# Summing the last row of a row-sum kernel by two pair adds on VectorE, with the first sum carried into the second

## The chip, the cores and the metric

The kernel runs on one core of one Trainium2 chip. The metric is the device time of one execution in microseconds (us), lower is better. A row holds 1,024 fp32 numbers.

## The reference

```python
batch, seq, dim = 32, 512, 1024
x = np.random.randn(batch, seq, dim).astype(np.float32)

def reference(x):
    return np.sum(x, axis=-1).astype(np.float32)
```

16,384 rows are summed: 67.1 MB are read and 64 KB are written. Each of the 128 partitions gets 128 rows, in four blocks of 32.

## The kernel before

Seven tiles of 16 rows per partition are loaded and summed, nearly all on VectorE. The last 16 rows come in shrinking pieces (8, 4, 2 and 1 rows, then the last row in 640 and 384 elements), so that little work is left when the last byte lands. VectorE and ScalarE share these pieces.

```python
    def sum_act(v, acc):                       # ScalarE: sum of v into acc
        nc.scalar.activation(out=v, in_=v, func=COPY, accum_out=acc)

    def row_pairs_dve(xt, res, j, c):          # VectorE: 512 pairs of one row
        h = D // 2
        a, b = xt[:, j * D : j * D + h], xt[:, j * D + h : (j + 1) * D]
        nc.vector.tensor_tensor_reduce(
            out=a, in0=a, in1=b, scale=1.0, scalar=0.0, op0=ADD, op1=ADD,
            accum_out=res[:, c : c + 1],
        )
    # ... (seven tiles of 16 rows; loads of 8, 4, 2 and 1 rows into xt) ...
    nc.sync.dma_start(out=tail[:, 0:CUT], in_=x_b[:, last : last + CUT])          # CUT = 640
    nc.sync.dma_start(out=tail[:, CUT:D], in_=x_b[:, last + CUT : last + D])
    # ... (8 + 4 rows, halved between VectorE and ScalarE) ...
    i = cuts[2]
    rows_dve(xt, res, i, 1, c + i)                      # row 12: VectorE
    rows_act(xt, res, i + 1, 1, c + i + 1)              # row 13: ScalarE
    row_pairs_dve(xt, res, i + 2, c + i + 2)            # row 14: VectorE, by pairs
    nc.vector.tensor_reduce(                            # row 15, first 320
        out=tail[:, D : D + 1], in_=tail[:, 0 : CUT // 2], axis=X, op=ADD
    )
    sum_act(tail[:, CUT // 2 : CUT], tail[:, D + 1 : D + 2])   # row 15, next 320
    nc.vector.tensor_reduce(                            # row 15, 384 + the two sums
        out=res[:, n - 1 : n], in_=tail[:, CUT : D + 2], axis=X, op=ADD
    )
    nc.sync.dma_start(out=out_b, in_=res)
```

## Time and profile before

| | before |
|---|---|
| time, median of 3 | 163.21 us (163.21 to 163.22) |
| the profiled execution | 163.75 us, span 162.0 us |
| read | 67.11 MB at 415 GB/s over the span |
| VectorE / ScalarE busy | 76% / 10% |

The page of the kernel before, its busy time and the share of the data movers in 40 slices of the span (a digit is the busy share in tenths):

```profile
DVE 123.5 (76%) x14; ACT 15.8 (10%) x29; POOL 0.2 (0%) x4
...
DMA  7979989989979969969959959969969959999991
```

The loads run nearly from start to end, and VectorE waits for each full tile (2.1 to 2.5 us for each after the first, by its timeline). What can still be shortened by compute is mainly the time between the landing of the last bytes and the issue of the final store.

The timeline of the last microseconds (start, length, engine, line, operation; in brackets the idle time before and what ended it):

```profile
157.86 0.69 DVE L57 CUSTOM_DVE_ANT_0 xt<-xt 128x512 f32<-128x512 f32 x1
158.48 0.08 DVE L57 DVE_READ_ACCUMULATOR2_ANT res<- 128x1 f32 x1
158.58 0.47 ACT L48 ACTIVATE tail<-tail 128x320 f32<-128x320 f32 x1 [0.97 <-DMA tail<-in_x_dram]
158.58 0.49 DVE L102 TENSOR_REDUCE tail<-tail 128x1 f32<-128x320 f32 x1
158.95 0.19 ACT L48 ACTIVATION_READ_ACCUMULATOR tail<-tail 128x1 f32 x1
159.17 0.55 DVE L106 TENSOR_REDUCE res<-tail 128x1 f32<-128x386 f32 x1
159.75 0.35 SPq L109 DMA_DIRECT2D out_dram<-res  x1
```

```profile
122.25 36.30 DMA tail<-in_x_dram
158.55 0.02 issue
158.58 0.47 ACT tail L48
159.05 0.10 ACTq L135
159.15 0.02 issue
159.17 0.55 DVE res L106
```

The first piece of the last row lands at 158.55 us, ScalarE sums half of it, and only then can VectorE's last reduction start. The second piece, by the trace's record of its landing at 159.014 us, is there earlier than ScalarE's sum. The store is issued at 159.75, that is 0.740 us after the last landing. This distance, from the last landing to the store's issue within one trace, is the first measure used below: it hardly depends on how the stream ran before (0.740 and 0.732 us in two traces of this kernel whose spans differ by 0.5 us; before_copy, below).

### The profile page before, as it was taken

What the parts mean: (1) busy time and instruction counts of PE and PEld (TensorE: products, weight loads), DVE (VectorE), ACT (ScalarE), POOL (GpSimd) and SP (SyncE); (2) the same over time, 40 slices, a digit from 0 to 9 for tenths busy, and PEclk for the clock granted to TensorE, in tenths of its full rate; (3) what the DMA queues carried; (4) which work ended last, traced back from release to release, by engine and by line L of the source; (5) the groups of instructions that cost most, each with busy time, mean ns of one, the idle gap of its engine ahead of it and who ended that gap; (6) DMA issues with size and microseconds to landing.
All of it is one profiled execution on the core that took longest, in us unless ns stands there. A gap on an engine that the chain in (4) does not pass through costs nothing.

```text
span 162.0 us, 116 instructions
## 1 busy us (share of the span) xinstructions
DVE 123.5 (76%) x14; ACT 15.8 (10%) x29; POOL 0.2 (0%) x4
## 2 busy tenths in 40 slices
DVE  0000039998699967999499994999949998599994
ACT  0000000000000000000000000000000000991881
POOL 0000000000000000000000000000000000000000
DMA  7979989989979969969959959969969959999991
GB/s 259 518 324 453 518 356 421 518 388 388 518 340 437 518 275 502 519 259 519 519 259 518 518 259 518 519 259 519 519 260 518 518 259 518 389 398 443 405 410 35
DMA packets 2448, 67.18 MB, mean 415 GB/s; under 512 B 784, under 2 KB 912, under 8 KB 1168
## 3 DMA queue, kind: packets, MB, share of 16 engines
q1 hardware_dynamic: 2016, 67.13, 96.6%
q10 hardware_dynamic: 432, 0.05, 0.2%
HBM read 67.11 MB, written 0.07 MB: 415 GB/s over the span
## 4 chain that ended last, share of the span: by engine, by line
DMA 76%; DVE 22%; ACT 0%; issue 0%; ACTq 0%
DMA xt<-in_x_dram 39%; DMA tail<-in_x_dram 22%; DVE res L40 21%; DMA out_dram<-res 15%; DVE res L106 0%; ACT tail L48 0%; ACTq L135 0%
## 5 line engine op out<-in xcount | busy, mean ns | idle before, releaser
L40 DVE TENSOR_REDUCE res<-xt 128x16 f32<-128x16384 f32 (+4 forms) x10 | 121.8, 12203 | 36.0 <-DMA xt<-in_x_dram 36.0
L48 ACT ACT_TABLE_LOAD x1 | 1.3, 1283 | 137.7 <-DVE res L40 137.7
L48 ACT ACTIVATE xt<-xt 128x1024 f32<-128x1024 f32 x13 | 13.6, 1045 | 4.7 <-DMA xt<-in_x_dram 4.7
L48 ACT ACTIVATION_READ_ACCUMULATOR xt<-xt 128x1 f32 x13 | 2.4, 186 | 0.0
L57 DVE CUSTOM_DVE_ANT_0 xt<-xt 128x512 f32<-128x512 f32 x1 | 0.7, 693 | 0.1
L106 DVE TENSOR_REDUCE res<-tail 128x1 f32<-128x386 f32 x1 | 0.6, 554 | 0.1
L48 ACT ACTIVATE tail<-tail 128x320 f32<-128x320 f32 x1 | 0.5, 469 | 1.0 <-DMA tail<-in_x_dram 1.0
L102 DVE TENSOR_REDUCE tail<-tail 128x1 f32<-128x320 f32 x1 | 0.5, 486 | 0.0
L48 ACT ACTIVATION_READ_ACCUMULATOR tail<-tail 128x1 f32 x1 | 0.2, 187 | 0.0
L124 POOL MEMSET const-bfloat16-1.0<- 128x1 bf16 x1 | 0.1, 102 | 0.0
L124 POOL MEMSET const-uint8-127<- 128x1 uint8 x1 | 0.1, 101 | 0.0
L124 POOL MEMSET const-float32-0.0<- 128x1 f32 x1 | 0.1, 99 | 0.2 <-issue 0.2
L124 POOL MEMSET const-float32-1.0<- 128x1 f32 x1 | 0.1, 98 | 0.0
L57 DVE DVE_READ_ACCUMULATOR2_ANT res<- 128x1 f32 x1 | 0.1, 83 | 0.0
## 6 DMA issues: line engine op xcount, KB each, us to landing
xt<-in_x_dram SPq DMA_DIRECT2D x1, 4096.0 KB, 31.2
xt<-in_x_dram SPq DMA_DIRECT2D x1, 2048.0 KB, 35.7
xt<-in_x_dram SPq DMA_DIRECT2D x1, 1024.0 KB, 37.7
xt<-in_x_dram SPq DMA_DIRECT2D x1, 512.0 KB, 38.5
tail<-in_x_dram SPq DMA_DIRECT2D x1, 320.0 KB, 36.3
tail<-in_x_dram SPq DMA_DIRECT2D x1, 192.0 KB, 36.4
xt<-in_x_dram SPq DMA_DIRECT2D x7, 41.2
out_dram<-res ACTq DMA_DIRECT2D x3, 16.0 KB, 23.7
```

The costliest lines, as they stand in the source:

```text
L40: nc.vector.tensor_reduce(out=res[:, c : c + n], in_=xt[:, j * D : (j + n) * D].rearrange("p (j d) -> p j d", d=D), axis=X, op=ADD,)
L48: nc.scalar.activation(out=v, in_=v, func=COPY, accum_out=acc)
L57: nc.vector.tensor_tensor_reduce(out=a, in0=a, in1=b, scale=1.0, scalar=0.0, op0=ADD, op1=ADD, accum_out=res[:, c : c + 1],)
L102: nc.vector.tensor_reduce(out=tail[:, D : D + 1], in_=tail[:, 0 : CUT // 2], axis=X, op=ADD)
L106: nc.vector.tensor_reduce(out=res[:, n - 1 : n], in_=tail[:, CUT : D + 2], axis=X, op=ADD)
L124: nc = _bacc.Bacc("TRN2", target_bir_lowering=False, num_devices=1)
```

## The change

The last row is cut at 576 instead of 640. Both pieces are added by pairs on VectorE, and the first sum is the starting value of the second. Thus ScalarE has no part in the last row, and it takes the row above whole. Two small reductions and a hand-over between engines give way to two short instructions. The core of the diff:

```diff
-CUT = 640
+CUT = 576
...
-    tail = rpool.tile([P, D + 2], F32, name="tail")
+    part = rpool.tile([P, 1], F32, name="part")
...
+    def pairs_dve(xt, a, b, first, acc):
+        h = (a + b) // 2
         nc.vector.tensor_tensor_reduce(
-            out=a, in0=a, in1=b, scale=1.0, scalar=0.0, op0=ADD, op1=ADD,
-            accum_out=res[:, c : c + 1],
+            out=xt[:, a:h], in0=xt[:, a:h], in1=xt[:, h:b], scale=1.0, scalar=first,
+            op0=ADD, op1=ADD, accum_out=acc,
         )
...
-    nc.sync.dma_start(out=tail[:, 0:CUT], in_=x_b[:, last : last + CUT])
-    nc.sync.dma_start(out=tail[:, CUT:D], in_=x_b[:, last + CUT : last + D])
+    last = 15 * D
+    for i, k in ((0, CUT), (CUT, D)):
+        nc.sync.dma_start(
+            out=xt[:, last + i : last + k],
+            in_=x_b[:, c * D + last + i : c * D + last + k],
+        )
...
-    row_pairs_dve(xt, res, i + 2, c + i + 2)
-    nc.vector.tensor_reduce(
-        out=tail[:, D : D + 1], in_=tail[:, 0 : CUT // 2], axis=X, op=ADD
-    )
-    sum_act(tail[:, CUT // 2 : CUT], tail[:, D + 1 : D + 2])
-    nc.vector.tensor_reduce(
-        out=res[:, n - 1 : n], in_=tail[:, CUT : D + 2], axis=X, op=ADD
-    )
+    rows_act(xt, res, 14, 1, c + 14)
+    pairs_dve(xt, last, last + CUT, 0.0, part)
+    pairs_dve(xt, last + CUT, last + D, part, res[:, c + 15 : c + 16])
     nc.sync.dma_start(out=out_b, in_=res)
```

The last row also moves from a tile of its own into the tile of the rows above it. Below, before and after stand for the two kernels, and "add one" and "add two" for the two pair adds of the last row.

## The prediction

> **What bounds the kernel now.** The load stream. The page shows 67.11 MB read in a span of 162.0 us. In the 40 slices the DMA row stands at 5 to 9 tenths throughout, while VectorE is busy 76% and ScalarE 10%. VectorE waits 2.1 to 2.5 us for a load before each full tile (timeline). So only what happens after the last bytes land can be shortened by compute. The chain of waits ends like this: the 640-element piece of the last row lands at 158.55 us; ScalarE sums its second half (158.58, 0.47 us, plus the accumulator read, ending about 159.14); VectorE sums the 386 leftovers (159.17, 0.55 us, ending 159.72); the store is issued at 159.75. The 384-element piece, issued 122.62 and 36.4 us on the way, lands about 159.0, so it is not what the final reduction waits for. VectorE frees at 158.56, ScalarE had idled 1.0 us from 157.6.

> **What the change does.**
> - Row 14 (the row above the last) leaves VectorE's pair add (693 ns, 157.86 to 158.55) for ScalarE (1.04 to 1.06 us, plus about 0.1 us for the accumulator read's end). It lands about 157.7; ScalarE then ends about 158.9. Off the chain.
> - The ScalarE hop in the last row (about 0.6 us) and both small reductions (486 and 554 ns) go. Two pair adds come, of 288 and 224 pairs.
> - [...] The accumulator read (83 ns) overlaps its add and ends about 15 ns after it.
> - The first piece has 64 elements per partition less (33 KB). At the 421 GB/s at which the two-row piece came in it lands some 0.08 us earlier. The second piece still ends the stream at about 159.0.

> **The new chain (estimates).** Piece one lands 158.47; add one 158.50 to 158.97. Piece two lands about 159.0. Add two also needs the first sum as a pointer scalar[...]. I allow 0.06 us for that wait, as the trace shows 0.06 us between the last one-row reduction and the pair add, and 0 to 0.06 us for the scalar operand. Add two starts 159.03 to 159.06 and ends 159.43 to 159.53. The store is issued about 159.5 instead of 159.75: 0.2 to 0.3 us gained. All else (stream, store's 1.4 us, end) stays. So 163.21 becomes about 162.97 us, 0.15% faster.

> **Chances.** Faster by over 2%: 0.005; within 2%: 0.99; slower by over 2%: 0.005. Range 162.75 to 163.20.

> **What would show it.** Chain of waits: its end is the load of the second piece, or of the first piece and then two pair adds; no ScalarE. Groups: pair adds of about 457 and 391 ns; ScalarE's 13 whole-row sums become 14. Timeline: VectorE idle about 0.65 us before add one; store issued near 159.5. Landing of the last piece unchanged within 0.1 us.

> **What would make it wrong.** The carried sum may cost more than 0.1 us between the two adds, eating half of the gain. Row 14 could land later than I read, so that ScalarE ends after 159.4 and becomes the last wait. The load stream itself could run differently (the last-row pieces now go to the rotating tile; their issue waits for a store before, 2.6 us, hidden by about 36 us of queued loads), which would move everything by more than the gain.

The sum: add two starts 0.03 to 0.06 us after the landing at 159.0, takes about 0.39 us and 0 to 0.06 us more for the pointer, and its accumulator read ends about 0.015 us later; that is the end at 159.43 to 159.53, the store at about 159.5 in place of 159.75, and so 162.97 us. The trace of before gives nearly the same lengths, as an estimate: VectorE's whole tiles take 17.22 us for 16,384 numbers per partition, 1.051 ns each, and if a pair takes as long, 693 ns for 512 pairs become 458 ns for 288 and 390 for 224. Measured later: 459 ns (after) and 393 (imm). The 0 to 0.06 us for the pointer was the author's guess; ptr1 measured 55 to 62 ns. That add two waits for VectorE's semaphore is recorded in the trace of after (risen at 158.555 us, start at 158.615). The accumulator reads there, and in before, end 8 to 9 ns after their adds.

## The result and the profile after

| | before | after |
|---|---|---|
| time, median of 4 | 163.22 us (163.21 to 163.27) | 163.22 us (163.16 to 163.38) |
| span of the profiled execution | 162.0 us | 161.4 us |
| last landing to store | 0.740 us | 0.656 us |
| last landing to end of span | 2.962 us | 2.929 us |

The ratio is 1.0001 with a 95% interval of 0.9984 to 1.0019. Ratios here are the mean time of one kernel's fast runs over that of the other's from the same rounds, so not quite the ratio of the medians. The predicted 0.25 us doesn't show in the time, though this interval alone just reaches it (ratio 0.9985).

The two traces must not be compared by their spans. The profiled execution of before took 163.75 us, well above the timed ones, and that difference lies in the middle of the load stream. VectorE's timeline of before, then of after (fourth and seventh tile; the line of the seventh in after takes in the three reductions that follow it):

```profile
81.28 17.22 DVE L40 TENSOR_REDUCE res<-xt 128x16 f32<-128x16384 f32 x1 [2.50 <-DMA xt<-in_x_dram]
...
139.34 10.82 DVE L40 TENSOR_REDUCE res<-xt 128x10 f32<-128x10240 f32 x1 [2.11 <-DMA xt<-in_x_dram]
```

```profile
80.74 17.22 DVE L40 TENSOR_REDUCE res<-xt 128x16 f32<-128x16384 f32 x1 [2.17 <-DMA xt<-in_x_dram]
...
138.78 18.46 DVE L40 TENSOR_REDUCE res<-xt 128x10 f32<-128x10240 f32 x4 [2.09 <-DMA xt<-in_x_dram]
```

By the seventh tile before is already 139.34 - 138.78 = 0.56 us later, at a place where the two kernels are identical. The spans differ by 0.57 us in all, so hardly anything is left for the code that the change touches.

The timeline of after, for the same stretch as above:

```profile
157.21 1.06 ACT L48 ACTIVATE xt<-xt 128x1024 f32<-128x1024 f32 x1
158.08 0.46 DVE L56 CUSTOM_DVE_ANT_0 xt<-xt 128x288 f32<-128x288 f32 x1 [0.83 <-DMA xt<-in_x_dram]
158.17 0.19 ACT L48 ACTIVATION_READ_ACCUMULATOR xt<-xt 128x1 f32 x1
158.46 0.08 DVE L56 DVE_READ_ACCUMULATOR2_ANT part<- 128x1 f32 x1
158.62 0.45 DVE L56 CUSTOM_DVE_ANT_0 xt<-xt,part 128x224 f32<-128x224 f32 x1
158.99 0.08 DVE L56 DVE_READ_ACCUMULATOR2_ANT res<- 128x1 f32 x1
159.14 0.35 SPq L103 DMA_DIRECT2D out_dram<-res  x1
```

And its chain of waits:

```profile
121.86 36.08 DMA xt<-in_x_dram
157.93 0.03 issue
157.96 0.02 DVEq L56
157.98 0.10 issue
158.08 0.46 DVE xt L56
158.53 0.02 DVE part L56
158.56 0.06 issue
158.62 0.45 DVE xt L56
```

ScalarE is gone from the chain, as intended, and the lengths are near the predicted ones (459 ns against 457 for add one). What is new is "DVEq L56" and the "issue" around it: between the landing of the first piece (157.93) and the start of add one (158.08) lie 0.144 us, where the tail's reduction and ScalarE's sum had started 0.024 us after their landing in before. The group of line 56 names the instruction that sits there:

```profile
L56 DVEq EVENT_SEMAPHORE  x2: 21/21/21, 158.0 to 158.5; - x2
```

Two separate wait instructions stand in VectorE's queue, one before each add. The semaphores that the trace records with each instruction say why (a semaphore is raised by one engine or load and waited for by another: in before, VectorE's rose at 157.814 us, and the pair add that waits for it started at 157.860): each add waits for two, that of its load and that of VectorE's own progress. For add two the second one guards the read of the first sum (with scratch outputs it goes when that read goes: imm, below); for add one it goes when the add no longer overwrites its input tile (scratch, below). In all these cases the wait for the load stands in the separate instruction and the add itself waits for VectorE.

### The profile page after: what moved, and what is told of

It is laid out like the page before. It is cut to its first block, busy times and chain, and to the rows that moved or that the text cites. A ratio compares the mean times of both kernels' runs of the same rounds, so it can differ in the third digit from the quotient of the medians.

```text
span 161.4 us, 117 instructions
## 1 busy us (share of the span) xinstructions
DVE 122.7 (76%) x14; ACT 16.4 (10%) x29; POOL 0.2 (0%) x4
## 3 DMA queue, kind: packets, MB, share of 16 engines
HBM read 67.11 MB, written 0.07 MB: 416 GB/s over the span
## 4 chain that ended last, share of the span: by engine, by line
DMA 76%; DVE 22%; issue 0%; DVEq 0%
DMA xt<-in_x_dram 61%; DVE res L40 21%; DMA out_dram<-res 15%; DVE xt L56 1%; DVEq L56 0%; DVE part L56 0%; DVEq L129 0%
## 5 line engine op out<-in xcount | busy, mean ns | idle before, releaser
L48 ACT ACTIVATE xt<-xt 128x1024 f32<-128x1024 f32 x14 | 14.6, 1046 | 4.8 <-DMA xt<-in_x_dram 4.7
L56 DVE CUSTOM_DVE_ANT_0 xt<-xt 128x288 f32<-128x288 f32 x1 | 0.5, 459 | 0.8 <-DMA xt<-in_x_dram 0.8
L56 DVE CUSTOM_DVE_ANT_0 xt<-xt,part 128x224 f32<-128x224 f32 x1 | 0.5, 450 | 0.1
L56 DVE DVE_READ_ACCUMULATOR2_ANT part<- 128x1 f32 x1 | 0.1, 83 | 0.0
L56 DVE DVE_READ_ACCUMULATOR2_ANT res<- 128x1 f32 x1 | 0.1, 81 | 0.0
```

Of the source, the lines that this page charges most:

```text
L56: nc.vector.tensor_tensor_reduce(out=xt[:, a:h], in0=xt[:, a:h], in1=xt[:, h:b], scale=1.0, scalar=first, op0=ADD, op1=ADD, accum_out=acc,)
```

## The experiments

Theory W: the second semaphore of an add costs a separate wait instruction, and with it about 0.12 us between landing and start. Rival C: the custom pair add itself starts late after any wait. Rival R: add two is late because it reads a sum that was just written. A further theory, P, is that the pointer operand (the first sum) makes add two longer. Theory D says that the profiled execution of before had an unusually slow stream.

Landings are taken from the trace's landing record of each load. All times in this table are in us, from the traces:

| run | waits of add one, add two | add one starts after its landing | last operation starts after the last landing | its length | store after the last landing | end of span after the last landing |
|---|---|---|---|---|---|---|
| before | (reductions) | - | 0.159 | 0.554 | 0.740 | 2.962 |
| before_copy | (reductions) | - | 0.148 | 0.555 | 0.732 | 2.951 |
| after | 2, 2 | 0.144 | 0.134 | 0.450 | 0.656 | 2.929 |
| after_copy | 2, 2 | 0.143 | 0.133 | 0.450 | 0.656 | 2.933 |
| after_again | 2, 2 | 0.139 | 0.135 | 0.450 | 0.656 | 2.938 |
| tail_only | 1, 2 | 0.023 | 0.134 | 0.452 | 0.658 | 2.943 |
| scratch | 1, 2 | 0.023 | 0.140 | 0.450 | 0.663 | 2.943 |
| imm | 1, 1 | 0.023 | 0.023 | 0.393 | 0.488 | 2.769 |
| imm_two | 1, 2 | 0.024 | 0.140 | 0.392 | 0.602 | 2.886 |
| ptr1 | 2, 1 | 0.145 | 0.062 (add one busy) | 0.448 | 0.583 | 2.866 |
| fold | 1, 2 | 0.023 | 0.139 | 0.396 | 0.605 | 2.889 |
| best2 | 1, 1 | 0.022 | 0.022 | 0.446 | 0.539 | 2.821 |
| best2_again | 1, 1 | 0.024 | 0.023 | 0.445 | 0.537 | 2.821 |
| row_only | (reductions) | - | 0.353 | 0.553 | 0.933 | 3.158 |

The last column shows what the store's issue hides. From the landing of the final store to the end of the span, before, before_copy and row_only take 0.791 to 0.792 us, and all the others 0.853 to 0.855. The group of SyncE's wait instructions at the end of the program, in before and then in after, has one more:

```profile
L135 SPq EVENT_SEMAPHORE  x6: 17/28/857, 160.2 to 161.9; - x6
```

```profile
L129 SPq EVENT_SEMAPHORE  x7: 17/28/859, 159.5 to 161.3; - x7
```

One more of them comes after the store's landing in after. SyncE there waits for ScalarE's semaphore too; that this is the reason was not tested. So of the 0.076 to 0.084 us that after gains up to the store's issue, only 0.013 to 0.033 us is left at the end of the span.

### before_copy: the kernel before once more

No edit.

> The kernel before, unchanged, as a floor for the noise and for a second trace of it. Theory D (the profiled execution of before that the prediction was read from took 163.75 us against 163.21 timed, so about 0.5 us of stream was in that trace and not in the times): span about 161.4, VectorE's first partial tile starts about 138.8 us instead of 139.34, and the store is issued about 159.2 us, still about 0.74 us after the last piece lands. Rival (the kernel before always has that stream): span 162.0 again and the partial tile at 139.3. Ratio 1.000 within 0.001.

163.24 us median (163.11 to 163.85), ratio 1.0003 (0.999 to 1.0016); span 161.5 us. Its seventh tile started here:

```profile
138.87 10.82 DVE L40 TENSOR_REDUCE res<-xt 128x10 f32<-128x10240 f32 x1 [2.11 <-DMA xt<-in_x_dram]
```

Theory D holds: 138.87 and not 139.34, with the same program. The store came 0.732 us after the last landing, so after gains 0.732 - 0.656 = 0.076 us to 0.084 us up to the store's issue. The executions of one kernel spread over 0.7 us here; the difference sought is far below that.

### after_copy and after_again: the changed kernel once more

No edit; two chips.

> The changed kernel, unchanged, more rounds. From its trace the store is issued 0.656 us after the last piece lands, against 0.740 in the kernel before: 0.08 us or 0.05 % gained. Expected ratio 0.9995, interval within 0.998 to 1.001; if the prediction's 0.25 us were there the ratio would be 0.9985. In the trace: add one starts 0.14 us after its piece lands, add two 0.13 us after its own, 450 ns long.

> The changed kernel again, on whichever chip this is, as its two comparisons so far gave 1.0001 and 1.0015. If the 0.0015 was scatter of the load stream: ratio within 0.999 to 1.001. If the changed kernel has a slower stream of its own: 1.001 to 1.002 again, with its last landing later than that of the kernel before.

After_copy: 163.56 us median (163.06 to 163.85), ratio 1.0015 (1.0002 to 1.0029). After_again: 163.12 us median (163.03 to 163.72), ratio 0.9991 (0.9971 to 1.0011). The expectation of after_copy missed: its interval lies above 1, where 0.9995 was expected. After_again's 0.9991 lies in the range expected if that was scatter, at its lower edge. All three traces have the store at 0.656 us. The 1.0015 didn't come back, so it is taken for scatter of the load stream. The 16 runs of after in the three comparisons average 163.32 us (4 x 163.248, 6 x 163.472, 6 x 163.213); the 26 runs of before beside them 163.33 us. The times can't resolve a few hundredths of a microsecond; the distances within a trace can.

### scratch: the adds don't overwrite their input

```diff
+        junk = rpool.tile([P, h - a], F32, name=f"junk{a}")
         nc.vector.tensor_tensor_reduce(
-            out=xt[:, a:h], in0=xt[:, a:h], in1=xt[:, h:b], scale=1.0, scalar=first,
+            out=junk, in0=xt[:, a:h], in1=xt[:, h:b], scale=1.0, scalar=first,
```

> After, with both pair adds writing their elementwise sums to scratch tiles in place of the input tile. Add one then waits for its load alone (before: for its load and for VectorE itself); add two still waits for two. Theory W (a second semaphore costs a separate wait instruction and with it about 0.12 us between landing and start): add one starts 0.02 to 0.03 us after its piece lands, with no separate wait instruction before it; add two still 0.13 us after its own piece. Theory C (the custom pair add always starts late): add one still 0.14 us after landing. Both: store 0.62 to 0.66 us after the last landing, for add two holds the end; time within 0.1 us of after. Results right.

163.26 us median (163.15 to 163.80), ratio 1.0006 (0.9995 to 1.0017). The two adds in its timeline, and the group of their line:

```profile
158.03 0.46 DVE L57 CUSTOM_DVE_ANT_0 junk<-xt 128x288 f32<-128x288 f32 x1 [0.71 <-DMA xt<-in_x_dram]
...
158.68 0.45 DVE L57 CUSTOM_DVE_ANT_0 junk<-xt,part 128x224 f32<-128x224 f32 x1 [0.19 <-DMA xt<-in_x_dram]
```

```profile
L57 DVEq EVENT_SEMAPHORE  x1: 21/21/21, 158.6 to 158.6; - x1
```

Add one lost its wait for VectorE, its separate wait instruction is gone, and it starts 0.023 us after its landing in place of 0.144. The same custom operation on the same data: rival C falls. (That it no longer writes in place isn't the reason: in ptr1, below, it writes to scratch too, has two waits again and is late again.) Add one now ends 0.11 us earlier relative to the last landing, and yet add two starts no earlier (0.140 against 0.134). So in after too it was the landing of the second piece, plus the two-wait start, that held add two. The chain of waits of after had named add one there, since add one's semaphore rose 0.025 us after the separate wait instruction had ended; only the experiment tells them apart. In after, add one would have held add two nearly as long: its semaphore rose 0.074 us after the last landing, and with the 0.023 us of a start with one wait that makes 0.097 us by estimate, against 0.134.

### tail_only and row_only: one half of the change each

tail_only leaves the row above on VectorE:

```diff
-    rows_act(xt, res, 14, 1, c + 14)
+    pairs_dve(xt, 14 * D, 15 * D, 0.0, res[:, c + 14 : c + 15])
```

> After, but the row above stays on VectorE as a pair add, so only the last row's treatment changes. Its landing is 1.30 us before the last; it starts about 0.14 us later (two waits), takes 0.69 us, ends about 0.45 us before the last landing, so add one starts there, about 0.1 us after its piece landed, and ends 0.05 to 0.1 us after the last landing. Store 0.68 to 0.75 us after the last landing (after: 0.656): moving the row to ScalarE is worth 0.02 to 0.1 us. Time within 0.1 us of after.

163.22 us median (163.12 to 163.36), ratio 0.9998 (0.9986 to 1.001); store at 0.658 us. The expectation (0.68 to 0.75) missed: with the row pair in front, add one had one wait only, started 0.023 us after its landing, while the row pair was still reading its accumulator, and ended 0.07 us before the last landing. So leaving the row on VectorE changes nothing in the tail (0.658 against 0.656).

row_only moves only the row, from the kernel before:

```diff
-    row_pairs_dve(xt, res, i + 2, c + i + 2)
+    rows_act(xt, res, i + 2, 1, c + i + 2)
```

> The kernel before, with only the row above moved to ScalarE. ScalarE ends that row about 0.12 us before the last landing, then sums its half of the 640 piece (0.47 plus 0.09 us), ends about 0.44 us after the last landing; the final reduction starts about 0.47 and ends about 1.03 us, store about 1.05 us after the last landing: 0.31 us later than before. So the move alone costs, and is free only together with the other half of the change.

One run, 163.38 us; store at 0.933 us, so 0.2 us later than before (0.732 to 0.740). The expected 0.31 was too much, since ScalarE's next sum overlaps the accumulator read of the one before (the read runs from 158.13 to 158.32 us, the next sum starts at 158.22). The direction holds: ScalarE comes late to its half of the last row, and the last reduction waits for it.

This run also bounds theory W. The last reduction of the kernel before waits for three semaphores. Here its separate wait instruction, for the load and for VectorE, had ended at 158.53 us; the reduction itself waited for ScalarE:

```profile
158.58 0.19 ACT L48 ACTIVATION_READ_ACCUMULATOR tail<-tail 128x1 f32 x1
158.80 0.55 DVE L106 TENSOR_REDUCE res<-tail 128x1 f32<-128x386 f32 x1 [0.32 <-ACT tail L48]
```

It started 0.025 us after ScalarE's semaphore rose (0.024 and 0.023 in before and before_copy). So more semaphores are not dear by their number alone: no delay shows where the wait that ends last stands on the instruction itself.

### imm, ptr1 and imm_two: the parts of add two's cost

All three give wrong results for the last row of each group, on purpose. They start from the kernel of the run scratch. imm starts add two from 0.0 and not from the first sum:

```diff
-    pairs_dve(xt, last + CUT, last + D, part, res[:, c + 15 : c + 16])
+    pairs_dve(xt, last + CUT, last + D, 0.0, res[:, c + 15 : c + 16])
```

> Scratch outputs, and add two starts from an immediate 0 and not from the first sum: its result for the last row of each group is wrong on purpose. Add two then waits for its load alone and has no pointer operand. Theory W: it starts 0.02 to 0.03 us after its landing, takes about 391 ns, store about 0.49 us after the last landing (after: 0.656). Rival (the start is late because of the first sum's read after write or of the custom operation): as scratch ruled the operation out for add one, it should not stay at 0.13.

The lengths without a pointer in this and the later expectations (391, 392 and 442 ns for 224, 225 and 273 pairs) are within 2 ns of an estimate from two traces: 693 ns for 512 pairs in before and 459 for 288 in after make 1.045 ns a pair, so 392, 393 and 443 ns. Measured were 393 (imm), 396 (fold) and 446 (best2).

Add two starts 0.023 us after the last landing, takes 393 ns, store at 0.488 us. There is no separate wait instruction left. The end of its chain of waits:

```profile
158.40 0.02 issue
158.43 0.39 DVE junk L57
```

imm takes away three things at once: a wait, the read of the fresh sum, and the pointer operand. imm_two puts back the wait alone, by letting both adds write to one scratch tile:

```diff
+    shared = rpool.tile([P, D // 2], F32, name="junk")
     def pairs_dve(xt, a, b, first, acc):
         h = (a + b) // 2
-        junk = rpool.tile([P, h - a], F32, name=f"junk{a}")
+        junk = shared[:, 0 : h - a]
```

> As imm (wrong for the last row on purpose), but both adds write their elementwise sums to one scratch tile, so add two has to wait for add one as well as for its load, with no pointer operand and no read of the first sum. Theory W: add two starts 0.13 to 0.14 us after its landing (imm: 0.023), 391 to 393 ns, store 0.60 us after the last landing (imm: 0.488). Rival (the late start in after came from reading the first sum): 0.02 to 0.03 us and 0.49 us.

Its chain of waits:

```profile
158.55 0.03 issue
158.58 0.02 DVEq L59
158.60 0.09 issue
158.69 0.39 DVE junk L59
```

The 0.02 us before the add become 0.03 + 0.02 + 0.09, and the store goes from 0.488 to 0.602 us: 0.114 us for one more semaphore, though that semaphore rose 0.025 us before the load landed. Nothing reads the first sum in this kernel, so rival R falls, and theory W holds for these adds, in which the load's wait, the last to end, stands in the separate instruction. No run has an add with the two waits the other way round. What inside the queue takes the 0.09 us after the wait instruction isn't shown by these traces.

ptr1 gives both adds a pointer to a tile of zeros, set long before:

```diff
+    zero = rpool.tile([P, 1], F32, name="zero")
+    nc.vector.memset(zero, 0.0)
...
-    pairs_dve(xt, last, last + CUT, 0.0, part)
-    pairs_dve(xt, last + CUT, last + D, part, res[:, c + 15 : c + 16])
+    pairs_dve(xt, last, last + CUT, zero, part)
+    pairs_dve(xt, last + CUT, last + D, zero, res[:, c + 15 : c + 16])
```

> As imm, but both adds start from a [P,1] tile of zeros set at the kernel's start (wrong for the last row on purpose). Add one waits for two (load, VectorE), add two for its load alone, both have the pointer operand. Pointer theory: 288 pairs take about 518 ns and not 459, 224 pairs about 450; add one starts 0.12 to 0.14 us after its landing, add two 0.02 to 0.03 after its own unless add one is still busy; store about 0.55 us after the last landing. Rival (the 59 ns come from reading a sum that was just written): 459 and 391 ns.

The two adds in its timeline:

```profile
158.10 0.52 DVE L59 CUSTOM_DVE_ANT_0 junk<-xt,zero 128x288 f32<-128x288 f32 x1 [0.84 <-DMA xt<-in_x_dram]
...
158.54 0.45 DVE L59 CUSTOM_DVE_ANT_0 junk<-xt,zero 128x224 f32<-128x224 f32 x1
```

Add one takes 519 ns with the pointer and 457 to 460 without; add two 448 and 392 to 393. So the pointer costs 55 to 62 ns, also where its value is a constant set at the start: theory P holds. Add one, with two waits again, starts 0.145 us late again; that kept VectorE busy beyond the last landing, so add two started at 0.062 us and the store came at 0.583, not the 0.55 that holds only if VectorE is free.

### fold and best2: the two costs taken out, with right results

fold keeps the last row in a tile of its own with two more columns: the first sum lands behind the data, next to a zero, and add two runs over 225 pairs without a pointer.

```diff
-    part = rpool.tile([P, 1], F32, name="part")
+    tail = rpool.tile([P, D + 2], F32, name="tail")
+    nc.vector.memset(tail[:, D + 1 : D + 2], 0.0)
...                                   (last row loaded into tail, junk as in scratch)
+    pairs_dve(tail, 0, CUT, 0.0, tail[:, D : D + 1])
+    pairs_dve(tail, CUT, D + 2, 0.0, res[:, c + 15 : c + 16])
```

> Right results. The first sum is written behind the last row's data, next to a zero, and add two takes 225 pairs over data, sum and zero in place of the pointer operand; it still waits for two. Add two 392 ns long, starts 0.13 to 0.14 us after the last landing; store 0.60 us after it (after 0.656, before 0.735).

One run, 163.24 us, right; add two 396 ns, store at 0.605 us: as expected.

best2 is fold with the cut at 480 and a one-element copy between the adds:

```diff
-CUT = 576
+CUT = 480
...
     pairs_dve(tail, 0, CUT, 0.0, tail[:, D : D + 1])
+    seen = rpool.tile([P, 1], F32, name="seen")
+    nc.vector.tensor_copy(out=seen, in_=tail[:, D : D + 1])
     pairs_dve(tail, CUT, D + 2, 0.0, res[:, c + 15 : c + 16])
```

The copy's result is not used. It waits for VectorE, in time that is idle anyway (158.27 to 158.42 us, with the load landing at 158.45), and the trace then records add two with its load as the only wait.

> Right results. As fold, with pieces of 480 and 544 and a one-element copy that reads the first sum between the two adds, so the copy takes the wait for VectorE and add two waits for its load alone. If the copy takes under 0.16 us: add one ends 0.22 us before the last landing, the copy by about 0.0, add two starts 0.02 to 0.05 us after the landing, takes 442 ns, store 0.53 to 0.57 us after the last landing. That is 0.17 to 0.2 us better than before, ratio 0.9989, which the rounds may not resolve (intervals so far 0.001 wide each way); the trace does.

> Fold with the copy between the adds, again, for the time: the trace says 0.2 us or 0.12 % less than before, the first comparison gave 0.9993 (0.9977 to 1.0009). Expected 0.9988 to 0.9995; store about 0.54 us after the last landing again.

The adds and the copy in best2's timeline:

```profile
157.82 0.41 DVE L58 CUSTOM_DVE_ANT_0 junk<-tail 128x240 f32<-128x240 f32 x1 [0.52 <-DMA tail<-in_x_dram]
...
158.27 0.15 DVE L105 COPY seen<-tail 128x1 f32<-128x1 f32 x1
158.47 0.45 DVE L58 CUSTOM_DVE_ANT_0 junk<-tail 128x273 f32<-128x273 f32 x1
```

Add two starts 0.022 us after the last landing (158.45), and the store comes at 0.539 and 0.537 us. That is 0.12 us better than after and 0.2 us better than before; at the end of the span 0.11 to 0.12 us and 0.13 to 0.14 us. In time: 163.21 us median (163.04 to 163.34), ratio 0.9993 (0.9977 to 1.0009), and on another chip 163.02 us (162.93 to 163.59), ratio 0.9991 (0.9968 to 1.0014). Both are near the 0.9992 that 0.13 to 0.14 us would give, and both intervals hold 1: by time alone it isn't proven faster. Nor do the times part it from after, whose ratio in the same rounds as best2_again was 0.9991 too. By the traces, the gain is just under 0.1%.

## Why the prediction was wrong

- **Right: the bound.** The load stream bounds the kernel (VectorE waited 2.1 to 2.5 us for each full tile after the first), and only the tail after the last landing was at stake. The class "within 2%" was right too.
- **Right: the structure.** ScalarE left the chain; the row above ended 0.13 us before the last landing; the first piece landed 0.549 us before the second (0.53 predicted); add one took 459 ns (457 predicted). Measured are 693, 459 and, in imm, 393 ns for 512, 288 and 224 pairs.
- **Wrong: "add one 158.50 to 158.97" from a landing at 158.47, and "add two starts 159.03 to 159.06" from one at 159.0.** The starts were reckoned 0.03 to 0.06 us after the landings; they were 0.144 and 0.134. This is the step that failed first. The runs show two semaphores per add, with the load's wait in a separate instruction, and 0.11 to 0.12 us for that (scratch, imm_two). The prediction had named the carried sum's wait as a risk for add two; for add one it reckoned with none.
- **Misread: the 0.06 us "between the last one-row reduction and the pair add".** It was taken for the price of a wait. But that pair add's load was issued at 119.17 us and landed at 157.716 (record of its landing), and the add started at 157.860: 0.144 us, the same two-wait start (0.139 in before_copy). The number that would have corrected the prediction stood in the trace of before; the reduction had ended in the meantime and hid it.
- **Under-weighted: the pointer operand, "0 to 0.06 us".** It cost 55 to 62 ns (ptr1), the top of that range.
- **Under-weighted: the store's issue.** It followed the end of the last accumulator read after 0.064 us in after, and the end of the reduction after 0.027 us in before. The trace records three semaphores for the store in place of two. In after VectorE's, the last to rise, stands in the separate wait instruction, and the store follows its rise by 0.053 us; in before it stands on the store itself, and the store follows by 0.016 us. That looks like theory W on SyncE, but no run changed it alone, so it stays open.
- **Wrong: "All else (stream, store's 1.4 us, end) stays".** The store's landing still came 1.42 to 1.43 us after its issue, but from there to the end of the span it took 0.853 us in after against 0.792 in before. This second failed step cost 0.06 us; SyncE's extra wait instruction stands there, and its cause stays open.
- **The sum.** Predicted: store about 0.5 us after the last landing (159.5 against 159.0). Later start 0.09 us (0.134 against the middle of 0.03 to 0.06), pointer 0.03 us above the middle of its range, store 0.04 us: 0.5 + 0.16 = 0.66, measured 0.656. So the store came 0.08 us earlier where 0.2 to 0.3 were expected, and the longer end took 0.06 of that back: 0.013 to 0.033 us were gained in all, too little for the times to show.
- **The range.** It ended at 163.20 us, just below the time of before, and so left no room for no gain at all. Single executions of before ran from 163.00 to 163.91 us in later rounds; the three first times, within 0.01 us of each other, had suggested a far smaller scatter.

## What to carry to other kernels

In a tail of a few tenths of a microsecond, look at the semaphores that each instruction waits for, and at which of them stands in a separate wait instruction, not only at its length: where the load's wait stood there, one more semaphore cost 0.11 us here, even though it was up in time. Let an instruction that has slack take the other wait (an output to scratch in place of the input tile: 0.023 us from landing to start and not 0.144, in scratch; or a tiny copy in idle time: 0.022 and not 0.134, in best2), and try passing a small sum as one more data element rather than as a pointer operand (396 ns against 450 here). Measure to the end of the span, not only to the last store's issue. Before reading a gap as the price of a wait, compare the start with the landing of the load that it waited for, and before promising 0.1%, run the unchanged kernel often enough to know its scatter.
